# A hybrid decoder layer on one core: five queues in written order, low halves over the landed words, and first weight sums made in HBM scratch

## The chip, the cores and the metric

The kernel runs on one core of a Trainium2 chip. The metric is the device time of one launch in microseconds, as the median of several runs. A profiled execution (a span, and a row for each instruction) stands beside it.

## The reference

One decoder layer over 256 positions of 2048 features. The input is normalised and multiplied by one wide matrix, whose columns are cut into nine parts; two branches mix the positions; a gated sum of both goes through an output matrix. All of it is in float32.

```python
h = rms_norm(x, norm_g)
q, k, v, z_a, u_b, v_b, z_b, g_a, g_b = split(h @ w_in)      # 7 x 1024 and 2 x 2048 columns
q = rms_norm(q by heads of 128); k = rms_norm(k by heads of 128)
att = causal attention(q, k, v)                              # 8 heads, 256 positions
y_a = (att * silu(z_a)) @ w_proj_a
sgu = spatial_gating(gelu(u_b), gelu(v_b))                   # u * (tril(W_s) @ norm(v) + b)
y_b = (sgu * silu(z_b)) @ w_proj_b
merged = sigmoid(g_a) * y_a + sigmoid(g_b) * y_b
return x + merged @ w_out
```

## The kernel before

All weights come as 120 units of 1 MB, each 128 partitions by 2048 words, in the order of their use. A unit of the input matrix holds one pair of row blocks (the number `kp`, 0 to 7) by 1024 output columns, as four blocks of 128 x 512 that are called 12, 11, 22 and 21 and lie in that order. Blocks of units follow one another: q, k, v, za, vb, ub, zb (8 units each), then four times a block g0 to g3 (8 units: half the columns from g_a, half from g_b) and its projections (`proj`, 4 units), then out0 and out1 (8 units each).

A float32 product is made of reduced words: a value is split into a high half (`fp32r`, the word rounded) and a low half (the word minus its high half), and a product is three matmuls of 512 columns: high by low, high by high, low by high (`three`, L290). A unit is multiplied in one of two ways. *Direct*: eight block products, 24 matmuls. *By seven*: seven products of sums of blocks, as in Strassen's and Winograd's schemes, 21 matmuls, for which sums of the weight blocks (`t`) and sums of the activations (`Fx`, `Fm`, and `F4` for kp 4) are made. In `k` to `zb` and in `out` the units with kp 0 to 3 go by seven, in g0 to g3 those with kp 0 to 4; q and the projections are direct.

`split` (L128 to L157) prepares a unit on two engines. Direct: ACT casts the words to `wh` (L125), DVE subtracts, `wl` (L126). By seven: DVE makes four sums `t` (L143 two at once, L145, L146), ACT casts three blocks (`whp`, L152) and the sums (`th`, L154, two pieces), DVE subtracts for `wlp` (L155) and `tl` (L157, two pieces). The words of a unit and its sums lie in the same five buffers. In the body of unit i the kernel writes load(i+3), split(i+2), the unit's matmuls, and then the small work of the branches: norms (`sums`: ACT squares, DVE L243, POOL's power L244, and for k a multiply by `rstd` on DVE, L369), transposes, softmax, the spatial mixing, and sums out of PSUM. Loads go from SP's queue, powers and masks to POOL. ACT's and DVE's instructions stand in written order for the first eight units only; behind these, and on the other engines throughout, a scheduler sets the order.

`turn_m` turns the merged activations for `out`: PE transposes, ACT copies and casts (L490), DVE subtracts (L491). The functions:

Of the kernel before, what the change touches and what calls it, by code (L numbers as in the profile page):

```python
# [45 lines left out]
PLAIN = (0, 1, 2, 3, 4, 5, 6, 7)  # L46
NVEC = KT + 2 + H


def schedule():  # L50
    s = []

    def quad(name, c, order):
        s.extend(("quad", name, c, kp, n) for n, kp in enumerate(order))

    quad("q", 0, PLAIN)
    for name in ("k", "v", "za", "vb", "ub", "zb"):
        quad(name, 0, MIXED)
    for c in range(4):
        quad("g", c, GATE)  # L60
        s.extend(("proj", "proj", c, q, q) for q in range(4))
    for c in range(2):
        quad("out", c, OUT[c])
    return s
# [3 lines left out]
def hybrid_layer_kernel(  # L68
# [12 lines left out]

    const = ctx.enter_context(tc.tile_pool(name="const", bufs=1))
# [4 lines left out]
    psum = ctx.enter_context(tc.tile_pool(name="psum", bufs=1, space=bass.MemoryType.PSUM))  # L87

# [13 lines left out]

    raw, wh, wl, th, tl = {}, {}, {}, {}, {}

    def strassen(i):
        if i >= NG or G[i][0] != "quad" or G[i][1] == G[0][1]:
            return False
        return G[i][3] in SK or (G[i][1] == "g" and G[i][3] == 4)

# [3 lines left out]
    def new_raw(i):  # L113
        raw[i] = wpool.tile([P, WORDS], F32, tag="raw", bufs=5, name=f"raw{i}")
# [13 lines left out]
    def split(i, pieces=1, js=None):  # L128
        if i >= NG:
            return  # L130
        r = raw[i]
        if not strassen(i):
            if i not in wh:
                wh[i] = wpool.tile([P, WORDS], F32R, tag="wh", bufs=3, name=f"wh{i}")
                wl[i] = wpool.tile([P, WORDS], F32R, tag="wl", bufs=3, name=f"wl{i}")
            n = WORDS // pieces
            for j in js or range(pieces):
                sl = slice(j * n, (j + 1) * n)
                halve(wh[i][:, sl], wl[i][:, sl], r[:, sl])
            return  # L140
        t = wpool.tile([P, WORDS], F32, tag="raw", bufs=5, name=f"t{i}")
        two = t[:, 0:2 * B].rearrange("p (a n) -> p a n", a=2)
        nc.vector.tensor_tensor(two, r[:, B:3 * B].rearrange("p (a n) -> p a n", a=2),  # L143
                                r[:, None, 0:B].to_broadcast([P, 2, B]), op=ALU.add)
        nc.vector.tensor_tensor(t[:, 2 * B:3 * B], t[:, 0:B], r[:, 2 * B:3 * B], op=ALU.add)  # L145
        nc.vector.tensor_tensor(t[:, 3 * B:], t[:, 2 * B:3 * B], r[:, 3 * B:], op=ALU.add)  # L146
        wh[i] = wpool.tile([P, 3 * B], F32R, tag="whp", bufs=3, name=f"whp{i}")
        wl[i] = wpool.tile([P, 3 * B], F32R, tag="wlp", bufs=2, name=f"wlp{i}")
        th[i] = wpool.tile([P, WORDS], F32R, tag="wh", bufs=3, name=f"th{i}")
        tl[i] = wpool.tile([P, WORDS], F32R, tag="wl", bufs=3, name=f"tl{i}")  # L150
        a, b = slice(0, 2 * B), slice(2 * B, WORDS)
        nc.scalar.copy(wh[i], r[:, B:])  # L152
        for sl in (a, b):
            nc.scalar.copy(th[i][:, sl], t[:, sl])  # L154
        nc.vector.tensor_tensor(wl[i], r[:, B:], f(wh[i]), op=ALU.subtract)  # L155
        for sl in (a, b):
            nc.vector.tensor_tensor(tl[i][:, sl], t[:, sl], f(th[i][:, sl]), op=ALU.subtract)  # L157
# [7 lines left out]

    xv = const.tile([P, NVEC + S], F32, name="xv")
    vec = xv[:, 0:NVEC]
# [8 lines left out]
    nc.sync.dma_start(xv, xT[:, 0:NVEC + S])  # L176
# [3 lines left out]
    load_piece(0, 2 * B, WORDS)  # L180
    load_x(2, 4)
    load(1, pieces=2)
# [22 lines left out]
    def split_x(kp, js=None):  # L205
        i, a = kp // 4, 2 * (kp % 4)
        for j in js or range(2):
            src = xv[:, NVEC:] if kp + j == 0 else xt[i][:, a + j, :]
            nc.scalar.activation(xt[i][:, a + j, :], src, AF.Copy, scale=vec[:, 2 * kp + j:2 * kp + j + 1])
# [8 lines left out]
    nc.gpsimd.memset(mhalf, -0.5)  # L218
    ninf = const.tile([P, 1], F32, name="ninf")
# [9 lines left out]
    def load_mix():  # L229
        X["ws"] = [u(f"ws{c}") for c in range(2)]  # L230
        for c in range(2):
            t = heads(X["ws"][c])
            nc.sync.dma_start(t, wsT[:, 4 * c:4 * c + 4, :])
            nc.gpsimd.affine_select(out=t, in_=t, pattern=[[0, 4], [1, P]], base=0,
                                    channel_multiplier=-1, compare_op=ALU.is_ge, fill=0.0)
        nc.sync.dma_start(gain, bass.AP(tensor=sg.tensor, offset=sg.offset, ap=[[0, P], [1, P]]))
# [22 lines left out]

    def halves_4():  # L260
# [3 lines left out]
    def forms(src, name):  # L264
        Fs = slot(F32, f"F{name}").rearrange("p (a k t) -> p a k t", a=4, t=P)
# [28 lines left out]
    def direct(L, hs, ls, i, kp, start, stop):  # L294
# [5 lines left out]
        for c, kh in order:  # L300
# [7 lines left out]
    def seven(E, L, i, kp, first, last, started, hs, ls, Fh, Fl):  # L308
# [18 lines left out]

        for acc, (hi, lo), (bh, bl) in ((L[0], A(1, 0), W("21")), (L[1], Fm(3), W("22")), (E[0], A(0, 0), W("11")),
                                       (E[3], Fm(0), T(0)), (E[2], Fm(2), T(1)), (E[1], Fm(1), T(2)),
                                       (L[2], A(1, 1), T(3))):  # L330
            three(acc, hi, lo, bh, bl, first if any(acc is e for e in E) else not started, last and any(acc is e for e in E))

    def early(E, name, res=None):

        c11, h, c22, c12 = (u(f"{name}_{n}") for n in ("c11", "h", "c22", "c12"))
# [21 lines left out]
    def sums(C, name):  # L357
        for m in range(2):
            for c in range(2):
                ss = small.tile([P, 4], F32, tag="ss", bufs=8, name="ss")  # L360
                junk = u("junk")
                scale = rstd[:, m:m + 1] if name == "k" else 1.0
                for h in range(4):
                    nc.scalar.activation(junk[:, h * P:(h + 1) * P], C[m][c][:, h * P:(h + 1) * P], AF.Square,
                                         scale=scale, accum_out=ss[:, h:h + 1])
                rs = small.tile([P, 4], F32, tag="rs", bufs=8, name="rs")
                rsqrt(rs, ss, 4, P)
                if name == "k":
                    nc.vector.tensor_scalar(rs, rs, scale, None, op0=ALU.mult)  # L369
                X["rs", name, m, c] = rs  # L370

    def norm_qk(name):
        C = X[name]
        for m in range(2):
            for c in range(2):
                for h in range(4):
                    sl = C[m][c][:, h * P:(h + 1) * P]
                    nc.scalar.activation(sl, sl, AF.Copy, scale=X["rs", name, m, c][:, h:h + 1])

    def norm_v():  # L380
        C = X["vb"]
        for m in range(2):
            for c in range(2):
                for h in range(4):
                    sl = C[m][c][:, h * P:(h + 1) * P]
                    nc.scalar.activation(sl, sl, AF.Copy, scale=X["rs", "vb", m, c][:, h:h + 1])
                t = heads(C[m][c])
                nc.vector.tensor_tensor(t, t, gain[:, None, :].to_broadcast([P, 4, P]), op=ALU.mult)
# [372 lines left out]
```

## Time and profile before

| what | value |
|---|---|
| median of 3 runs | 660.44 us (660.41 to 662.72) |
| profiled execution | 660.26 us, of which the span is 658.5 us |
| PE busy | 650.4 us, 2980 matmuls |
| DVE busy | 606.3 us, 606 instructions |
| ACT busy | 427.8 us, 564 instructions |
| POOL busy | 25.3 us, 26 instructions |
| moved from HBM | 132.7 MB, one queue at 55.4% |

A row of the timeline gives the start, the duration, engine, line, operation and tiles, and in brackets how long the engine sat idle before it and who released it. A row of groups gives the count, the busy time in us, the mean of one in ns, and behind the second bar the idle time before. Matmuls are pipelined: the start of the next row, not the duration, is the price of one.

### The profile page before, as it was taken

How to read it: one execution, taken by the hardware profiler on the slowest of the kernel's cores; microseconds unless marked ns; L12 is line 12 of the kernel's file. 1: busy time of each engine (PE TensorE's matmuls, PEld its weight loads, DVE VectorE, ACT ScalarE, POOL GpSimd, SP SyncE). 2: the span in 40 equal slices, each digit the busy share in tenths (PEclk: the TensorE clock that was granted, in tenths of full speed). 3: DMA queues.
4: the chain of work that ended last, by engine and by line, in shares of the span. 5: the costliest groups of instructions: out<-in, count | busy, mean ns of one | idle time of the engine just before them, and what ended most of it. 6: DMA issues, size and time to landing. Idle time of an engine off the chain costs nothing.

```text
span 658.5 us, 7820 instructions
## 1 busy us (share of the span) xinstructions
PE 650.4 (99%) x2980; PEld 538.7 (82%) x2980; DVE 606.3 (92%) x606; ACT 427.8 (65%) x564; POOL 25.3 (4%) x26
## 2 busy tenths in 40 slices
PE   8999999999999999999999999999999999999997
PEld 5888887888888888888888888888888888888886
DVE  5879997999999799999999999899799979998995
ACT  7889779658886589675655755556474546746360
POOL 1002203000000003000000000000000000000000
PEclk9999999999999999999999999999999999999999
DMA  8975643652664456456449436834755483557641
GB/s 312 420 311 209 261 153 129 255 193 86 236 222 161 163 188 219 165 192 230 153 159 351 137 127 264 302 130 190 266 183 192 137 319 130 189 190 282 198 153 64
DMA packets 22213, 135.32 MB, mean 205 GB/s; under 512 B 2464, under 2 KB 3104, under 8 KB 7072
## 3 DMA queue, kind: packets, MB, share of 16 engines
q1 hardware_dynamic: 21024, 132.73, 55.4%
q10 hardware_dynamic: 1152, 2.10, 0.9%
q8 instruction: 23, 0.38, 0.2%
q14 instruction: 14, 0.11, 0.1%
HBM read 132.72 MB, written 2.10 MB: 205 GB/s over the span
## 4 chain that ended last, share of the span: by engine, by line
PE 93%; DVE 3%; POOL 1%; DMA 1%; issue 1%; ACT 0%; SPq 0%; DVEq 0%
PE acc_g L290 16%; PE y L290 13%; PE acc_out L290 9%; PE seven_g L290 8%; PE acc_q L290 6%; PE acc_vb L290 5%; PE acc_za L290 5%; PE acc_ub L290 5%; PE acc_zb L290 5%; PE acc_k L290 4%; PE seven_out L290 3%; PE acc_v L290 2%; PE seven_vb L290 2%; PE seven_zb L290 2%; PE seven_ub L290 2%; PE seven_za L290 2%
## 5 line engine op out<-in xcount | busy, mean ns | idle before, releaser
L126 DVE TENSOR_TENSOR wl<-raw,wh 128x2048 fp32r<-128x2048 f32 (+2 forms) x76 | 156.2, 2062 | 27.7 <-ACT wh L125 27.3
L154 ACT CAST th<-t 128x1024 fp32r<-128x1024 f32 x104 | 107.7, 1055 | 102.0 <-DVE t L146 35.3
L125 ACT CAST wh<-raw 128x2048 fp32r<-128x2048 f32 (+2 forms) x76 | 130.9, 1730 | 60.2 <-issue 25.3
L157 DVE TENSOR_TENSOR tl<-t,th 128x1024 fp32r<-128x1024 f32 x104 | 125.2, 1222 | 2.9 <-ACT th L154 2.9
L155 DVE TENSOR_TENSOR wlp<-raw,whp 128x1536 fp32r<-128x1536 f32 x52 | 91.0, 1750 | 1.2 <-ACT whp L152 1.2
L152 ACT CAST whp<-raw 128x1536 fp32r<-128x1536 f32 x52 | 76.8, 1482 | 23.6 <-DMA raw<-in_w 21.5
L143 DVE TENSOR_TENSOR t<-raw 128x1024 f32<-128x1024 f32 x52 | 63.3, 1218 | 1.8 <-DMA raw<-in_w 1.5
L290 PE MATMUL acc_g<-wh,xul 128*128 128x512 f32 x96 | 37.3, 389 | 0.0
L290 PE MATMUL acc_g<-wh,xuh 128*128 128x512 f32 x96 | 37.3, 389 | 0.0
L290 PE MATMUL acc_g<-wl,xuh 128*128 128x512 f32 x96 | 37.3, 389 | 0.0
L145 DVE TENSOR_TENSOR t<-t,raw 128x512 f32<-128x512 f32 x52 | 36.0, 691 | 0.2
L146 DVE TENSOR_TENSOR t<-t,raw 128x512 f32<-128x512 f32 x52 | 35.6, 685 | 0.4
L290 PE MATMUL acc_q<-wh,xuh 128*128 128x512 f32 x64 | 25.0, 391 | 1.2 <-ACT wh L125 1.2
L290 PE MATMUL acc_q<-wl,xuh 128*128 128x512 f32 x64 | 25.2, 395 | 0.3 <-DVE wl L126 0.2
L290 PE MATMUL y<-wh,zbl 128*128 128x512 f32 x64 | 25.1, 392 | 0.0
L290 PE MATMUL y<-wh,zal 128*128 128x512 f32 x64 | 25.0, 390 | 0.0
L290 PE MATMUL acc_q<-wh,xul 128*128 128x512 f32 x64 | 24.9, 390 | 0.0
L290 PE MATMUL acc_out<-wh,mh 128*128 128x512 f32 x64 | 24.9, 389 | 0.0
L290 PE MATMUL acc_out<-wl,mh 128*128 128x512 f32 x64 | 24.9, 389 | 0.0
L290 PE MATMUL y<-wl,zah 128*128 128x512 f32 x64 | 24.9, 389 | 0.0
L290 PE MATMUL y<-wh,zbh 128*128 128x512 f32 x64 | 24.9, 389 | 0.0
L290 PE MATMUL y<-wl,zbh 128*128 128x512 f32 x64 | 24.9, 389 | 0.0
(496 smaller groups left out, 1582.2 us busy)
## 6 DMA issues: line engine op xcount, KB each, us to landing
raw<-in_w SPq DMA_DIRECT2D x116, 1024.0 KB, 4.8
raw<-in_w SPq DMA_DIRECT2D x7, 512.0 KB, 8.1
xnat<-in_x SPq DMA_DIRECT2D x2, 1024.0 KB, 16.0
xres<-in_x ACTq DMA_DIRECT2D x8, 256.0 KB, 3.9
out<-out_c SPq DMA_DIRECT2D x5, 256.0 KB, 2.5
xt<-in_xT SPq DMA_DIRECT2D x2, 512.0 KB, 8.2
xt<-in_xT SPq DMA_DIRECT2D x3, 256.0 KB, 9.0
raw<-in_w SPq DMA_DIRECT2D x2, 256.0 KB, 4.3
```

Of the source, the lines that this page charges most:

```text
L125: nc.scalar.copy(h, r)
L126: nc.vector.tensor_tensor(l, r, f(h), op=ALU.subtract)
L143: nc.vector.tensor_tensor(two, r[:, B:3 * B].rearrange("p (a n) -> p a n", a=2), r[:, None, 0:B].to_broadcast([P, 2, B]), op=ALU.add)
L145: nc.vector.tensor_tensor(t[:, 2 * B:3 * B], t[:, 0:B], r[:, 2 * B:3 * B], op=ALU.add)
L146: nc.vector.tensor_tensor(t[:, 3 * B:], t[:, 2 * B:3 * B], r[:, 3 * B:], op=ALU.add)
L152: nc.scalar.copy(wh[i], r[:, B:])
L154: nc.scalar.copy(th[i][:, sl], t[:, sl])
L155: nc.vector.tensor_tensor(wl[i], r[:, B:], f(wh[i]), op=ALU.subtract)
L157: nc.vector.tensor_tensor(tl[i][:, sl], t[:, sl], f(th[i][:, sl]), op=ALU.subtract)
L290: nc.tensor.matmul(acc, a, b, start=(start and n == 0), stop=(stop and n == 2))
```

## The change

1. All five engines' queues stand in written order from the first unit to the last. Four tables set it: `SETS` (which units of a block go by seven, and the order of the eight), `LEADS` (how many units ahead a unit is split), `EVAC` and `SECOND` (when sums leave PSUM and when the second part of a turn is written), and `HOOKS` (84 entries: at which unit and at which point of it each small work is written).
2. Low halves are written over the landed words in the same bytes (an arena whose parts have two names, float32 and fp32r). Six word buffers and three sum buffers replace the five and the separate low halves. A load is written five units ahead and waits for the matmuls of the unit before the current one.
3. In g1, g2 and g3 the unit kp 5 goes by seven too (six units), in g0 only four. In out0 kp 0, 1, 2 and 4 go by seven. The activations' sums for kp 5 are `F5h` and `F5l` (`forms_5`), which out0 makes anew for its kp 4 from the turned columns (`forms_m4`, `halves_m4`).
4. The weight sums of a unit are written otherwise: the first, 12 + 11, lies in place of block 12. For the 46 units by seven of za, vb, ub, zb, g and out it is made in HBM: SP copies block 12 to one of twelve scratch tiles 13 units ahead (`pre_copy`), POOL's queue adds block 11 there with an accumulating DMA 10 units ahead (`pre_sum`), and the load takes 256 KB from scratch and 768 KB from the matrix. The other three sums are DVE rows of 512 words; ACT casts 2048 and 1536 words, DVE subtracts 2048 and 1536.
5. For k, the multiply by `rstd` is on ACT, a row of its own ahead of the norm. Unit 0's last half and unit 1 are loaded in pieces of 256 KB. The last sums out of PSUM (`early`) are written in another order.

```diff
-SK = (0, 1, 2, 3)
-MIXED = (4, 5, 0, 1, 6, 2, 3, 7)
-GATE = (5, 0, 1, 6, 2, 3, 4, 7)
-OUT = ((0, 1, 4, 2, 5, 3, 6, 7), (4, 0, 1, 5, 2, 3, 6, 7))
+SETS = {("q", 0): ((), (0, 1, 2, 4, 3, 5, 7, 6)), ("k", 0): ((0, 1, 2, 3), (4, 5, 1, 6, 0, 2, 3, 7)),
...
+        ("g", 1): ((0, 1, 2, 3, 4, 5), (0, 4, 5, 6, 3, 1, 2, 7)),
...
+        ("out", 0): ((0, 1, 2, 4), (3, 0, 1, 5, 2, 4, 6, 7)),
+        ("out", 1): ((0, 1, 2, 3), (4, 0, 5, 1, 2, 3, 6, 7))}
+SCRATCH = ("za", "vb", "ub", "zb", "g", "out")
+LEADS = {("q", 0): (3, 2, 2, 3, 3, 3, 2, 2), ("k", 0): (2, 2, 2, 2, 2, 2, 2, 2),
...
+HOOKS = [
+    ("v", 0, 2, "pre", "root", "k", 0), ("v", 0, 2, "pre", "squares", "k", 1),
...
+RAWS, WHS, THS, TS = 6, 4, 3, 3
...
+    words = [both(f"words{n}", WORDS, base + 8 * KB * n) for n in range(RAWS)]
+    sums = [both(f"sums{n}", 3 * B, base + 8 * KB * RAWS + 6 * KB * n) for n in range(TS)]
...
+    ctx.enter_context(tc.manual_schedule(engines=set(engines)))
...
+    def pre_copy(i):
+        if i < NG and strassen(i) and G[i][1] in SCRATCH:
+            pre[i] = ring[len(pre) % len(ring)]
+            nc.sync.dma_start(pre[i], w[i, :, 0:B])
+
+    def pre_sum(i):
+        if i in pre:
+            nc.gpsimd.dma_start(pre[i], w[i, :, B:2 * B], accum_op=ALU.add)
+
     def load(i, pieces=1):
...
+        if i in pre:
+            nc.sync.dma_start(raw[i][:, 0:B], pre[i])
+            load_piece(i, B, WORDS)
+            return
...
+        if i in pre:
+            nc.scalar.copy(wh[i], r)
+            mid()
+        else:
+            nc.scalar.copy(wh[i][:, B:], r[:, B:])
+            mid()
+            nc.vector.tensor_tensor(r[:, 0:B], r[:, 0:B], r[:, B:2 * B], op=ALU.add)
+            nc.scalar.copy(wh[i][:, 0:B], r[:, 0:B])
+        nc.vector.tensor_tensor(T2, r[:, 0:B], r[:, 2 * B:3 * B], op=ALU.add)
+        nc.vector.tensor_tensor(T1, T2, r[:, B:2 * B], op=ALU.subtract)
+        nc.vector.tensor_tensor(T3, T2, r[:, 3 * B:], op=ALU.add)
+        nc.scalar.copy(th[i], t)
+        late()
+        nc.vector.tensor_tensor(wl[i], r, f(wh[i]), op=ALU.subtract)
+        nc.vector.tensor_tensor(tl[i], t, f(th[i]), op=ALU.subtract)
...
+    def norm(name, n):
...
+        if name == "k":
+            nc.scalar.activation(rs, rs, AF.Copy, scale=rstd[:, m:m + 1])
...
-        if i:
-            load(i + 3)
-        split(i + 2, 2 if i < 2 else 1)
+        while i and loaded < i + RAWS - 1:
+            loaded += 1
+            load(loaded)
+        pre_copy(i + 13)
+        pre_sum(i + 10)
```

Three places show the order. In its rows a line number, the operation, and output <- inputs stand, with the number of a unit in the tile's name (`wl20` is unit 20's low half; after the change the tile is one of six, `words2`, and the unit is seen in `wh20`).

DVE in v, before, from the third quarter of k's norm to unit 20's low half:

```order
L243 TENSOR_SCALAR ms_945<-ss_938 128x4
L143 TENSOR_TENSOR t21_993<-raw21_960 128x1024
L369 TENSOR_SCALAR rs_944<-rs_944,rstd_128 128x4
L243 TENSOR_SCALAR ms_956<-ss_949 128x4
L145 TENSOR_TENSOR t21_993<-t21_993,raw21_960 128x512
L369 TENSOR_SCALAR rs_955<-rs_955,rstd_128 128x4
L146 TENSOR_TENSOR t21_993<-t21_993,raw21_960 128x512
L155 TENSOR_TENSOR wlp21_998<-raw21_960,whp21_997 128x1536
L126 TENSOR_TENSOR wl20_963<-raw20_876,wh20_962 128x2048
L157 TENSOR_TENSOR tl21_1000<-t21_993,th21_999 128x1024 x2
```

DVE at that place, after:

```order
L265 TENSOR_TENSOR words1float32r_58<-words1float32_57,wh19_932 128x2048
L266 TENSOR_TENSOR sums0float32r_92<-sums0float32_91,th19_933 128x1536
L358 TENSOR_SCALAR ms_974<-ss_926 128x4
L358 TENSOR_SCALAR ms_984<-ss_977 128x4
L230 TENSOR_TENSOR words2float32r_60<-words2float32_59,wh20_987 128x2048
L258 TENSOR_TENSOR words3float32_61<-words3float32_61 128x512
L260 TENSOR_TENSOR sums1float32_93<-words3float32_61 128x512
L261 TENSOR_TENSOR sums1float32_93<-sums1float32_93,words3float32_61 128x512
L262 TENSOR_TENSOR sums1float32_93<-sums1float32_93,words3float32_61 128x512
L265 TENSOR_TENSOR words3float32r_62<-words3float32_61,wh21_1024 128x2048
```

Unit 20's low half (L126, now L230) stood behind unit 21's sums and low half and behind two of the multiplies L369; now it stands ahead of unit 21, and the multiplies are not in this queue.

DVE in out0, before, from unit 106's low half (`ml` is a low half of the turned columns of the fourth gate block, which units with kp 4 and more need):

```order
L126 TENSOR_TENSOR wl106_4525<-raw106_4476,wh106_4524 128x2048
L491 TENSOR_TENSOR ml1_4461<-ps_mT30_4556,mh1_4460 128x4x128
L143 TENSOR_TENSOR t107_4580<-raw107_4522 128x1024
L155 TENSOR_TENSOR wlp107_4585<-raw107_4522,whp107_4584 128x1536
L491 TENSOR_TENSOR ml1_4461<-ps_mT31_4563,mh1_4460 128x4x128
L145 TENSOR_TENSOR t107_4580<-t107_4580,raw107_4522 128x512
L157 TENSOR_TENSOR tl107_4587<-t107_4580,th107_4586 128x1024
L146 TENSOR_TENSOR t107_4580<-t107_4580,raw107_4522 128x512
L126 TENSOR_TENSOR wl108_4618<-raw108_4578,wh108_4617 128x2048
L157 TENSOR_TENSOR tl107_4587<-t107_4580,th107_4586 128x1024
L143 TENSOR_TENSOR t109_4648<-raw109_4615 128x1024
```

DVE there, after, from the low halves of unit 106, which now goes by seven:

```order
L265 TENSOR_TENSOR words4float32r_64<-words4float32_63,wh106_4392 128x2048
L266 TENSOR_TENSOR sums0float32r_92<-sums0float32_91,th106_4393 128x1536
L230 TENSOR_TENSOR words5float32r_66<-words5float32_65,wh107_4428 128x2048
L397 TENSOR_TENSOR F4m_4431<-m4_4292 128x128
L398 SCALAR_TENSOR_TENSOR F4m_4431<-F4m_4431,m4_4292 128x128
L399 TENSOR_TENSOR F4m_4431<-m4_4292 128x128
L400 TENSOR_TENSOR F4m_4431<-m4_4292,F4m_4431 128x128
L260 TENSOR_TENSOR sums1float32_93<-words0float32_55 128x512
L261 TENSOR_TENSOR sums1float32_93<-sums1float32_93,words0float32_55 128x512
L262 TENSOR_TENSOR sums1float32_93<-sums1float32_93,words0float32_55 128x512
L265 TENSOR_TENSOR words0float32r_56<-words0float32_55,wh108_4459 128x2048
L266 TENSOR_TENSOR sums1float32r_94<-sums1float32_93,th108_4460 128x1536
```

Ahead of these rows stand, after the change, the two `ml` rows (L639) and three sums of unit 106; behind them come `F5l` (L677) and the five rows of unit 109. Before, units 106 and 108 were direct and the `ml` rows stood behind `wl106`.

SP's queue in v, after (before, it holds only whole loads, L111, one for each unit):

```order
L202 DMA words1float32_57<-in_w 128x2048
L221 DMA words2float32_59<-ring0_119 128x512
L202 DMA words2float32_59<-in_w 128x1536
L221 DMA words3float32_61<-ring1_120 128x512
L202 DMA words3float32_61<-in_w 128x1536
L210 DMA ring4_123<-in_w 128x512
L202 DMA words4float32_63<-in_w 128x2048
L210 DMA ring5_124<-in_w 128x512
L221 DMA words5float32_65<-ring2_121 128x512
```

POOL's queue at the same units, after (before, it holds the powers alone there):

```order
L359 TENSOR_TENSOR rs_694<-ms_695,mhalf_176 128x4
L214 DMA ring0_119<-in_w 128x512
L214 DMA ring1_120<-in_w 128x512
L359 TENSOR_TENSOR rs_973<-ms_974,mhalf_176 128x4
L359 TENSOR_TENSOR rs_983<-ms_984,mhalf_176 128x4
L214 DMA ring2_121<-in_w 128x512
L214 DMA ring3_122<-in_w 128x512
```

A load from scratch (L221) and one of 1536 words stand for a load of 2048; copies to scratch (L210) stand between loads, and POOL issues the additions (L214) between powers.

More of the change, by code (lines that the diff above doesn't have):

```diff
@@ L1 @@
+import inspect
+import re
 from contextlib import ExitStack
@@ L51, in schedule, with quad @@
     s = []
[L53 to L58, printed above, removed]
+    def quad(name, c):
+        s.extend(("quad", name, c, kp, n) for n, kp in enumerate(SETS[name, c][1]))
+    for name in ("q", "k", "v", "za", "vb", "ub", "zb"):
+        quad(name, 0)
     for c in range(4):
-        quad("g", c, GATE)
+        quad("g", c)
         s.extend(("proj", "proj", c, q, q) for q in range(4))
     for c in range(2):
-        quad("out", c, OUT[c])
+        quad("out", c)
     return s
@@ L99, in f @@
         return ap.bitcast(F32)
+    engines = (mybir.EngineType.SP, mybir.EngineType.Pool, mybir.EngineType.Activation, mybir.EngineType.DVE,
+               mybir.EngineType.PE)
+    ctx.enter_context(tc.manual_schedule(engines=set(engines)))
     raw, wh, wl, th, tl = {}, {}, {}, {}, {}
+    pre = {}
+    ring = [dram.tile([P, B], F32, tag=f"ring{n}", name=f"ring{n}") for n in range(12)]
     def strassen(i):
-        if i >= NG or G[i][0] != "quad" or G[i][1] == G[0][1]:
-            return False
-        return G[i][3] in SK or (G[i][1] == "g" and G[i][3] == 4)
+        return i < NG and G[i][0] == "quad" and G[i][3] in SETS[G[i][1:3]][0]
     def load_piece(i, a, b):
@@ L139, in split @@
                 halve(wh[i][:, sl], wl[i][:, sl], r[:, sl])
+            mid()
+            late()
             return
[L141 to L157, printed above, removed]
+        wh[i] = wpool.tile([P, WORDS], F32R, tag="wh", bufs=WHS, name=f"wh{i}")
+        th[i] = wpool.tile([P, 3 * B], F32R, tag="th", bufs=THS, name=f"th{i}")
+        t, tl[i] = sums[len(th) % TS]
+        T1, T2, T3 = (t[:, a * B:(a + 1) * B] for a in range(3))
+        if i in pre:
+            nc.scalar.copy(wh[i], r)
+            mid()
+        else:
+            nc.scalar.copy(wh[i][:, B:], r[:, B:])
+            mid()
+            nc.vector.tensor_tensor(r[:, 0:B], r[:, 0:B], r[:, B:2 * B], op=ALU.add)
[4 more added lines that the diff above has]
+        nc.scalar.copy(th[i], t)
+        late()
+        nc.vector.tensor_tensor(wl[i], r, f(wh[i]), op=ALU.subtract)
+        nc.vector.tensor_tensor(tl[i], t, f(th[i]), op=ALU.subtract)
     X = {}
@@ L179, in hybrid_layer_kernel @@
     load_x(1, 2)
-    load_piece(0, 2 * B, WORDS)
+    load_piece(0, 2 * B, 3 * B)
+    load_piece(0, 3 * B, WORDS)
     load_x(2, 4)
-    load(1, pieces=2)
+    load(1, pieces=4)
     load_x(4, 8)
@@ L292, in hybrid_layer_kernel, with direct @@
     BLK = {"12": 0, "11": 1, "22": 2, "21": 3}
-    def direct(L, hs, ls, i, kp, start, stop):
+    def direct(L, hs, ls, i, kp, start, stop, hook=None):
         t, a = kp // 4, 2 * (kp % 4)
@@ L299, in direct @@
             order = [(c, kh) for kh in range(2) for col in (1, 0) for c in (col, 2 + col)]
-        for c, kh in order:
+        for j, (c, kh) in enumerate(order):
+            if hook and j == 6:
+                hook()
             r, col = c // 2, c % 2
@@ L306, in direct, with seven @@
                   first=(i == 0))
-    def seven(E, L, i, kp, first, last, started, hs, ls, Fh, Fl):
+    def seven(E, L, i, kp, first, last, started, hs, ls, Fh, Fl, hook=None):
         a = 2 * (kp % 4)
@@ L354, in final @@
         return [[c11, c12], [h, c22]]
[L357 to L388, printed above, removed]
+    QUARTERS = ((0, 0), (1, 0), (0, 1), (1, 1))
@@ new lines, in squares, with root @@
+    def squares(name, n):
+        m, c = QUARTERS[n]
+        C = X[name][m][c]
+        ss = X["ss", name, n] = small.tile([P, 4], F32, tag="ss", bufs=8, name="ss")
+        junk = u("junk")
+        scale = rstd[:, m:m + 1] if name == "k" else 1.0
+        for h in range(4):
+            nc.scalar.activation(junk[:, h * P:(h + 1) * P], C[:, h * P:(h + 1) * P], AF.Square,
+                                 scale=scale, accum_out=ss[:, h:h + 1])
+    def root(name, n):
+        X["rs", name, n] = small.tile([P, 4], F32, tag="rs", bufs=8, name="rs")
+        rsqrt(X["rs", name, n], X["ss", name, n], 4, P)
@@ L619, in hybrid_layer_kernel @@
+    for block, c, n, when, fn, *a in HOOKS:
+        at(first[block, c] + n, fns[fn], *a, when=when)
     split_x(0, [0])
```

372 lines of the change are left out of this document (222 added, 150 removed), and 29 rows, old and new, of tables (HOOKS, LEADS, SETS).

## The prediction

> **What bounds the kernel now.** I read the page's busy times and chain first, then the list of what PE waited for, then PE's timeline at each wait and the other engines there.
>
> ```profile
> PE 650.4 (99%) x2980; PEld 538.7 (82%) x2980; DVE 606.3 (92%) x606; ACT 427.8 (65%) x564; POOL 25.3 (4%) x26
> PEclk9999999999999999999999999999999999999999
> PE 93%; DVE 3%; POOL 1%; DMA 1%; issue 1%; ACT 0%; SPq 0%; DVEq 0%
> ```
>
> ```profile
> PE acc_v L290 <- DVE wl L126: 1.3, 1, 1.3
> PE ps_w L203 <- DVE warm L200: 1.3, 1, 1.3
> PE acc_q L290 <- ACT wh L125: 1.2, 1, 1.2
> PE acc_q L290 <- DVE wl L126: 0.2, 1, 0.2
> ```
>
> PE is busy 99% of the span at full clock and 93% of the chain is PE. Its whole list of waits has four entries, three of them at the start or in the first block and one in v. So the time is the number of matmuls by their period, plus a start, a tail and two stalls. The period is read where nothing waits (first and last of 30 rows, 29 intervals):
>
> ```profile
> 205.38 0.39 PE L290 MATMUL seven_vb<-tl,Fhx 128*128 128x512 f32 x1
> ...
> 211.96 0.39 PE L290 MATMUL acc_vb<-th,xuh 128*128 128x512 f32 x1
> ```
>
> 6.58 / 29 = 0.2269 us; the second column (0.39) overlaps from row to row and is not the price. A direct unit is 24 x 0.2269 = 5.45 us, a unit by seven products 21 x 0.2269 = 4.76.
>
> DVE at 92% is the near second, so both are costed. The first stall, in v, and DVE ahead of it:
>
> ```profile
> 114.02 0.39 PE L290 MATMUL acc_v<-wh,xuh 128*128 128x512 f32 x1
> 115.73 0.51 PE L290 MATMUL acc_v<-wl,xuh 128*128 128x512 f32 x1 [1.32 <-DVE wl L126]
> 116.07 0.40 PE L290 MATMUL acc_v<-wh,xul 128*128 128x512 f32 x1
> ```
>
> ```profile
> 109.19 0.23 DVE L369 TENSOR_SCALAR rs<-rs,rstd 128x4 f32<-128x4 f32 x1 [0.90 <-POOL rs L244]
> ...
> 111.12 0.68 DVE L146 TENSOR_TENSOR t<-t,raw 128x512 f32<-128x512 f32 x1
> 111.72 1.75 DVE L155 TENSOR_TENSOR wlp<-raw,whp 128x1536 fp32r<-128x1536 f32 x1
> 113.39 2.28 DVE L126 TENSOR_TENSOR wl<-raw,wh 128x2048 fp32r<-128x2048 f32 x1
> ```
>
> ```profile
> L369 DVE TENSOR_SCALAR rs<-rs,rstd 128x4 f32<-128x4 f32 x4 | 0.9, 229 | 3.4 <-POOL rs L244 3.4
> ```
>
> Two intervals take 2.05 us instead of 0.45: 1.60 us are lost. The low half that PE waits for (unit 20, at 113.39) stands behind unit 21's sums and low half, and these behind four multiplies that each sit 0.9 us until POOL's power is done.
>
> The second stall, at unit 1, lies between these two rows (five intervals, 2.04 us instead of 1.13, so 0.91 lost), with ACT and DVE ahead of it:
>
> ```profile
> 12.04 0.39 PE L290 MATMUL acc_q<-wh,xuh 128*128 128x512 f32 x1
> ...
> 14.08 0.40 PE L290 MATMUL acc_q<-wh,xul 128*128 128x512 f32 x1
> ```
>
> ```profile
> 10.46 2.18 ACT L125 CAST wh<-raw 128x512 fp32r<-128x512 f32 x4
> 11.20 2.49 DVE L126 TENSOR_TENSOR wl<-raw,wh 128x512 fp32r<-128x512 f32 x4
> ```
>
> **The change part by part.** The sum is made against the profiled execution, 660.26 us; the median of the runs is 660.44, 0.18 above it.
>
> 1. *Fewer matmuls.* Units by seven products go from 52 to 54: g1, g2 and g3 have six instead of five, g0 four instead of five. Each saves three matmuls, 6 in all: 6 x 0.2269 = **-1.36 us**, wholly on the path as long as PE is fed.
>
> 2. *The v stall.* The order now has unit 20's low half right behind unit 19 and two small rows, ahead of unit 21; the multiply is on ACT, a unit later than the power. DVE gets back 3.4 us of waits and 4 x 0.23 of multiplies, and 4.3 us of unit 21's work no longer stand ahead: 8.6 us against the 1.60 lost. Next late would be unit 21, needed 5.45 us after unit 20, which has the same 4.3 freed. ACT takes over four small rows, each written a unit (4.76 us at least) after the power that it reads, so it doesn't wait there. **-1.60 us.** The other end, if ACT did wait 0.9 at each multiply and passed it on, is 0.
>
> 3. *DVE's work per unit.* The rows:
>
> ```profile
> L126 DVE TENSOR_TENSOR wl<-raw,wh 128x2048 fp32r<-128x2048 f32 x64 | 146.3, 2286 | 24.9 <-ACT wh L125 24.5
> L157 DVE TENSOR_TENSOR tl<-t,th 128x1024 fp32r<-128x1024 f32 x104 | 125.2, 1222 | 2.9 <-ACT th L154 2.9
> L155 DVE TENSOR_TENSOR wlp<-raw,whp 128x1536 fp32r<-128x1536 f32 x52 | 91.0, 1750 | 1.2 <-ACT whp L152 1.2
> L143 DVE TENSOR_TENSOR t<-raw 128x1024 f32<-128x1024 f32 x52 | 63.3, 1218 | 1.8 <-DMA raw<-in_w 1.5
> L145 DVE TENSOR_TENSOR t<-t,raw 128x512 f32<-128x512 f32 x52 | 36.0, 691 | 0.2
> ```
>
> Before, a unit by seven costs 1.22 + 2 x 0.69 + 1.75 + 2 x 1.22 = 6.79 us of DVE. After, with the first sum made in HBM: 3 x 0.69 + 2.29 (2048 words) + 1.75 (1536) = 6.11; without it (k and v) one 0.69 more, 6.80, no change. A direct unit costs 2.29 both times, so a sixth unit by seven adds 3.82 and five save 0.68 each: a g1-g3 block changes by 3.82 - 3.40 = +0.4. PE takes 61.9 us for each of two such blocks of before, and three matmuls, 0.68, less after, 61.2:
>
> ```profile
> 383.42:445.30 61.88, 61.88 (x275) 51.24 (x274) 59.52 (x56) 35.07 (x28) 0.00 (x0) 1.00 0.56 204
> 445.30:507.18 61.88, 61.88 (x275) 51.24 (x274) 55.41 (x51) 33.60 (x28) 0.00 (x0) 1.00 0.55 205
> ```
>
> (The columns are window, length, busy PE, PEld, DVE, ACT and POOL, clock, DMA share, GB/s.) DVE would have 59.9 and 55.8 of 61.2: still under PE. **0**; the cover is 1.3 us in the tighter block, and each further us of DVE there costs one.
>
> 4. *out0.* The order of units there makes a tight place. Let T be the start of its first unit, direct. PE needs unit 109's low half after that unit and eight transposes, two units by seven, a direct one, one by seven and two matmuls. The transposes:
>
> ```profile
> 559.05 0.60 PE L398 MATMUL ps_mT<-ident,g_c 128*128 128x128 f32 x4
> 559.49 0.60 PE L398 MATMUL ps_mT<-ident,g_h 128*128 128x128 f32 x4
> ```
>
> Four take 0.44, eight 0.88. That is T + 5.45 + 0.88 + 4.76 + 4.76 + 5.45 + 4.76 + 0.45 = T + 26.5. DVE can start unit 106 only behind the low halves of the turned columns: the transposes begin after 18 matmuls (T + 4.1), take 0.9, then ACT's copies and two DVE rows of 0.69, about T + 6.8. Then come units 106 and 108 whole (2 x 6.11), 107's low half (2.29), four small form rows, one 0.69 and unit 109 without its last row (4.36).
>
> ```profile
> L273 DVE TENSOR_TENSOR F<-xt 128x128 f32<-128x128 f32 x1 | 0.3, 284 | 0.0
> ```
>
> With 0.28 for a form row that is 12.22 + 2.29 + 1.14 + 0.69 + 4.36 = 20.7: ready at T + 27.5, 1.0 late. But rows overlap in the timeline (111.12 to 111.72 is 0.60 for a row of 0.68, 111.72 to 113.39 is 1.67 for 1.75); 18 rows with 0.09 less each take 19.1, ready at T + 25.9, in time. Ends 0 and 1.2; I take **+0.4**, nearer the spacing, which is what a queue that doesn't wait shows.
>
> 5. *The start.* Unit 1 comes in four pieces instead of two. But ACT's four casts run at 0.545 apiece without a gap, and DVE follows at 0.6, so a landing didn't set the stall: **0**. It can give at most the 0.9, and lose as much as a piece's cast, 0.5.
>
> 6. *DMA.* 46 units send 256 KB to a scratch ring, add 256 KB there from POOL's queue, and load it back in place of 256 KB; the copy and the addition come on top, 46 x 2 x 0.262 = 24.1 MB.
>
> ```profile
> q1 hardware_dynamic: 21024, 132.73, 55.4%
> raw<-in_w SPq DMA_DIRECT2D x116, 1024.0 KB, 4.8
> raw<-in_w SPq DMA_DIRECT2D x2, 256.0 KB, 4.3
> ```
>
> 132.73 MB take 55.4%, so 24.1 more take 10%, together 65%; if an addition, for which no row exists, costs twice a copy, 70%. A copy is written 3 units ahead of its addition (14.3 us) and that 5 ahead of the load (23.8) against a landing of 4.3. On SP a load waits for PE's unit i-1, and later copies stand behind it; on POOL the powers stand behind additions, each written a unit ahead of its reader. **0**; the cover is these leads.
>
> By the Trainium skill, "DMA: Bandwidth & Descriptors", section on the anatomy of a DMA on the SWDGE (gpsimd) path, a DMA from that queue takes about 2.0 us and its bytes at 436 GB/s; that makes an estimate of 2.6 us for an addition, and the sum would be the same. No run here shows it.
>
> 7. *POOL beside DVE.* The only place where both work on SBUF and DVE shows a long row:
>
> ```profile
> 196.20 2.26 POOL L234 TENSOR_SCALAR_AFFINE_SELECT ws<-ws 128x512 f32<-128x512 f32 x2 [85.25 <-ACT za_c L462]
> 195.18 2.79 DVE L157 TENSOR_TENSOR tl<-t,th 128x1024 fp32r<-128x1024 f32 x2
> 197.89 1.11 DVE L145 TENSOR_TENSOR t<-t,raw 128x512 f32<-128x512 f32 x1
> ```
>
> DVE's row of 0.69 took 1.11, 0.42 more, beside a POOL instruction of 1.13. If issuing an addition did the same, its price would lie between 0 and 1.13 us of DVE, 46 times. I take 0, as the row shows POOL computing on SBUF and an addition goes from HBM to HBM.
>
> By the Trainium skill, "SBUF — State Buffer", section "SBUF: two separate sides", the port pair of DVE and GpSimd is an exclusive lock, which a DVE operation with two SBUF inputs holds only against a GpSimd operation that reads SBUF. The trace agrees with the lock (0.42 us). The same section says that descriptors written by GpSimd are shut out while DVE runs in a two-port mode; there the DMA would be late and not DVE, and the sum stays.
>
> Sum: 660.26 - 1.36 - 1.60 + 0.4 = 657.7, and 0.18 for the median: **657.9 us**.
>
> **Rivals.**
>
> *R1, faster by over 0.5%.* The start's stall goes too (-0.9) since the smaller pieces let ACT begin earlier, and out0 holds (-0.4): 656.6. For it: the list of waits names ACT's cast there as well as DVE, and an earlier cast moves both. Against it: the casts run without a gap, so earlier words must also reach an ACT that is free earlier.
>
> *R2, the v stall only moves, or additions cost DVE the 0.42 seen.* With the stall, 659.5. With the additions: the tighter g block goes to 59.9 + 6 x 0.42 = 62.4 against 61.2, +1.2, and three additions in out0 +1.3: 660.4. For it: DVE at 92%. Against it: 8.6 us freed in v, and no SBUF in the addition.
>
> *R3, slower: each addition holds DVE.* At price x a block of g1-g3 needs 57.9 (the mean of the two) + 6x, out0 3x more: 3 x (57.9 + 6x - 61.2) + 3x over 657.9 passes 663.7 from x = 0.75 (0.5 if all blocks are like the tighter). At 1.13 it is 10.4 + 3.4 more, 671.7. For it: POOL has 26 instructions now, and nothing like these in the steady stretch. Against it: the only such row cost DVE 0.42.
>
> **How the numbers follow.** What a measurement can tell from no change is about 0.5%: below 657.1 is faster, above 663.7 slower. The forecast, with out0 between 0 and its end, has 0.53; R1 0.22, since 0.8 us separate the forecast from its bound and the start's and out0's terms together can give that; R2 0.13; R3 0.12. So faster 0.22, same 0.66, slower 0.12. The range goes from 656.0 (R1, and half of the 1.2 us that PE waits for ACT's cast in the first block) to 661.5 (R2's worst and out0's other end); R3 and the rest of R1 lie outside.
>
> **What would show it.** Right: 2974 matmuls instead of 2980; no PE wait in v; DVE rows of 0.69, 2.29 and 1.75 unchanged beside POOL's additions; the DMA share near 65%. The unit 1 stall still there at 0.9. In out0 PE waits for DVE's low half of the fifth or sixth unit by at most 1.2. Wrong: PE waits spread over g1-g3, behind DVE (R3) or behind a landing; a PE wait in v for another unit (R2); no wait at unit 1 (R1).

## The result, and the profile after

The changed kernel takes 670.62 us (median of 4 runs, 670.40 to 671.46) against 660.42: the ratio is 1.0148, 95% interval 1.0125 to 1.0172. The forecast was 657.9, within 656.0 and 661.5; what came is slower. The profiled execution took 671.46 us, 11.20 more than that of before. One execution of a later kernel, the profiled one of the first experiment, ran at a granted clock of 0.85 (726.90 us against 671.77 to 672.36 for the other three); no time below counts it, and that kernel has no period below. Three lines of the changed kernel's page, and its whole list of PE's waits:

```profile
PE 663.1 (99%) x2974; PEld 539.4 (81%) x2974; DVE 598.0 (89%) x577; ACT 425.8 (64%) x534; POOL 59.1 (9%) x72
PEclk9999999999999999999999999999999999999999
PE 98%; DMA 1%; ACT 0%; DVE 0%; SPq 0%; DVEq 0%; issue 0%
```

```profile
PE ps_w L314 <- DVE warm L311: 1.3, 1, 1.3
PE acc_q L416 <- ACT wh L229: 1.1, 1, 1.1
```

Six matmuls fewer, no wait in v, none in g or out0, full clock, 98% of the chain on PE: by these views the change did what it says. And yet PE is busy 12.7 us longer. The place to look is the spacing of the starts where nothing waits. Ten rows of PE's timeline in g1, after:

```profile
399.84 0.40 PE L416 MATMUL seven_g<-sums0float32r,xuh 128*128 128x512 f32 x1
400.07 0.39 PE L416 MATMUL acc_g<-th,xul 128*128 128x512 f32 x1
400.30 0.39 PE L416 MATMUL acc_g<-th,xuh 128*128 128x512 f32 x1
400.53 0.40 PE L416 MATMUL acc_g<-sums0float32r,xuh 128*128 128x512 f32 x1
400.77 0.39 PE L416 MATMUL acc_g<-wh,xul 128*128 128x512 f32 x1
400.99 0.39 PE L416 MATMUL acc_g<-wh,xuh 128*128 128x512 f32 x1
401.22 0.40 PE L416 MATMUL acc_g<-words4float32r,xuh 128*128 128x512 f32 x1
401.46 0.39 PE L416 MATMUL acc_g<-wh,F5l 128*128 128x512 f32 x1
401.69 0.39 PE L416 MATMUL acc_g<-wh,F5h 128*128 128x512 f32 x1
401.92 0.40 PE L416 MATMUL acc_g<-words4float32r,F5h 128*128 128x512 f32 x1
```

Nine intervals take 2.08 us, 0.231 each, where before 29 took 6.58, 0.2269. It is so from the first block to the last: behind the first 33 matmuls there are some 2670 intervals between 0.215 and 0.245 us, and their mean is 0.23166 us, before 0.22681. That is 2670 x 0.00485 = 12.95 us.

With this the difference adds up, to within the 0.2 us to which such terms can be read, from the starts of PE's rows. The last matmul starts at 665.04 instead of 654.14, +10.90. Longer period: +12.95. Six matmuls: -1.36. The v stall: -1.60. The first block: +0.75, below. A short gap in out0: +0.16 (two intervals of 0.279 and 0.334). Sum +10.9. The tail behind the last matmul adds 0.3, which brings the span to +11.2.

### The profile page after: what moved, and what is told of

It reads as the page before. It is cut to its first block, busy times and chain, and to the rows that moved or that the text cites. A ratio compares the mean times of both kernels' runs of the same rounds, so it can differ in the third digit from the quotient of the medians.

```text
span 669.7 us, 8157 instructions
## 1 busy us (share of the span) xinstructions
PE 663.1 (99%) x2974; PEld 539.4 (81%) x2974; DVE 598.0 (89%) x577; ACT 425.8 (64%) x534; POOL 59.1 (9%) x72
## 4 chain that ended last, share of the span: by engine, by line
PE 98%; DMA 1%; ACT 0%; DVE 0%; SPq 0%; DVEq 0%; issue 0%
PE acc_g L416 15%; PE y L416 13%; PE acc_out L416 9%; PE seven_g L416 9%; PE acc_q L416 7%; PE acc_k L416 5%; PE acc_v L416 5%; PE acc_vb L416 5%; PE acc_zb L416 5%; PE acc_za L416 5%; PE acc_ub L416 5%; PE seven_out L416 3%; PE seven_k L416 2%; PE seven_zb L416 2%; PE seven_vb L416 2%; PE seven_za L416 2%
## 5 line engine op out<-in xcount | busy, mean ns | idle before, releaser
L214 POOL DMA_DIRECT2D ring<-in_w x46 | 38.3, 846 | 400.4 <-DMA ring<-in_w 400.4
L263 ACT CAST th<-sums1float 128x1536 fp32r<-128x1536 f32 x18 | 26.8, 1487 | 51.3 <-DVE sums1float L262 51.3
L263 ACT CAST th<-sums0float 128x1536 fp32r<-128x1536 f32 x18 | 26.6, 1479 | 44.1 <-DVE sums0float L262 44.1
L230 DVE TENSOR_TENSOR words5float32r<-words5float,wh 128x2048 fp32r<-128x2048 f32 x14 | 32.0, 2286 | 3.6 <-ACT wh L229 3.6
L266 DVE TENSOR_TENSOR sums1float32r<-sums1float,th 128x1536 fp32r<-128x1536 f32 x18 | 31.5, 1753 | 3.2 <-ACT th L263 3.2
L230 DVE TENSOR_TENSOR words4float32r<-words4float,wh 128x2048 fp32r<-128x2048 f32 x13 | 29.7, 2287 | 4.4 <-ACT wh L229 4.4
L266 DVE TENSOR_TENSOR sums2float32r<-sums2float,th 128x1536 fp32r<-128x1536 f32 x18 | 31.5, 1752 | 0.2 <-ACT th L263 0.2
L266 DVE TENSOR_TENSOR sums0float32r<-sums0float,th 128x1536 fp32r<-128x1536 f32 x18 | 31.6, 1753 | 0.0
L265 DVE TENSOR_TENSOR words2float32r<-words2float,wh 128x2048 fp32r<-128x2048 f32 x12 | 27.5, 2292 | 1.2
L416 PE MATMUL acc_out<-wh,ml 128*128 128x512 f32 x72 | 28.3, 393 | 0.0
L230 DVE TENSOR_TENSOR words1float32r<-words1float,wh 128x2048 fp32r<-128x2048 f32 x9 | 20.6, 2287 | 5.5 <-ACT wh L229 5.5
```

The lines of the kernel that those rows point to most:

```text
L214: nc.gpsimd.dma_start(pre[i], w[i, :, B:2 * B], accum_op=ALU.add)
L230: nc.vector.tensor_tensor(l, r, f(h), op=ALU.subtract)
L263: nc.scalar.copy(th[i], t)
L265: nc.vector.tensor_tensor(wl[i], r, f(wh[i]), op=ALU.subtract)
L266: nc.vector.tensor_tensor(tl[i], t, f(th[i]), op=ALU.subtract)
L416: nc.tensor.matmul(acc, a, b, start=(start and n == 0), stop=(stop and n == 2))
```

## Experiments

Three theories were set against each other: the address of an operand matters (A); traffic and writes in place slow PE's reads (B); waits in PE's queue (C). Addresses and offsets are worked out from the sizes of the tiles, in the order in which the kernel makes them; the traces hold none. In a matmul of this kernel the stationary operand is a tile of activations and the moving operand, of 512 columns, a tile of weights.

**All operands on multiples of 64 bytes.** In the kernel before every operand of a matmul starts on a multiple of 64; in the changed one the activations and high halves start 32 past it.

```diff
-    rstd = const.tile([P, 2], F32, name="rstd")
-    ssum = const.tile([P, 2], F32, name="ssum")
+    pair = const.tile([P, 4], F32, name="pair")
+    rstd, ssum = pair[:, 0:2], pair[:, 2:4]
```

> The changed kernel with rstd and ssum in one tile of the const pool, so that every later tile starts 32 bytes lower and every operand of a matmul starts on a multiple of 64 bytes, as in the kernel before; nothing else differs. Theory A (matmul operands that start 32 bytes past a multiple of 64 lengthen the issue period from 0.2267 to 0.2317 us): about 2650 matmuls get 0.005 us back, 13 us, so about 657.5 us, and the steady rows show 0.2267 again. Rival B (20% more DMA traffic and low halves written over the landed words slow PE's reads): no change, 670.6 us. Rival C (waits between matmuls in PE's queue): no change, 670.6 us.

671.78 us, ratio 1.0173 (1.0156 to 1.0190): no gain.

**The kernel before, shifted as a whole** by the same edit:

> The kernel before with rstd and ssum in one tile of the const pool, so that every later tile starts 32 bytes lower: nearly all matmuls then have both operands 32 bytes past a multiple of 64. Nothing else differs. Theory A: about 2670 matmuls at 0.2317 us or a little more instead of 0.2267, 13 us or more, so 673 us or above. Rivals B and C: no change, 660.4 us.

660.59 us, ratio 1.0001 (0.9992 to 1.0010), mean period 0.2268. Theory A in this form is dead: with both operands 32 bytes past a multiple of 64 the period is that of before.

**Only stationary, or only moving operands off the line:**

```diff
     small = ctx.enter_context(tc.tile_pool(name="small", bufs=4))
+    wpool.tile([P, 8], F32, tag="gap", bufs=1, name="gap")
```

(in the changed kernel, with three buffers instead of four for the small tile `mx`; and in the kernel with the one-tile edit above)

> The changed kernel with 32 bytes set in ahead of the casts of the weights (and one small buffer fewer), so that the moving operands (wh, th, low halves) all start on a multiple of 64 and only the stationary ones (activations) stay 32 past it. Theory A1 (the moving operand's address costs): about 657.5 us. Theory A2 (the stationary operand's address costs): about 670 us. Both: between, 661 to 668. Rivals B and C: 670.6 us.

> The changed kernel with all stationary operands on a multiple of 64 and the high halves and high sums of the weights (two thirds of the moving operands) 32 bytes past it. Theory A1 (the moving operand's address costs): about 670 us. Theory A2 (the stationary operand's address costs): about 657.5 us. Rivals B and C: 670.6 us.

675.42 us (ratio 1.0225, 1.0208 to 1.0242) and 671.15 (1.0172, 1.0144 to 1.0200); mean periods in the profiled executions 0.2333 and 0.2330. Each was expected to be fast under one half of theory A, and neither is. The first has a *longer* period than the changed kernel; so had the second in its profiled execution, which took 674.89 us, while its other three took 670.56 to 671.32. What made that one longer no run shows. What the two kernels share with it, and what the shifted kernel of before lacks, is that the two operands of a matmul stand at different offsets to each other: 32 and 288 bytes (modulo 512) in the one, 32 and 320 in the other, 288 for the low halves and sums in the changed kernel, 320 for these in the kernel aligned to 64. In the kernel before, shifted or not, all are 0. That this offset between the two operands sets the period is theory D, and it was tested in both directions.

**The changed kernel with equal offsets.** Instructions and their order are the same; only addresses move.

```diff
-    mhalf = const.tile([P, 8], F32, name="mhalf")
+    mhalf = const.tile([P, 80], F32, name="mhalf")
...
-        ss = X["ss", name, n] = small.tile([P, 4], F32, tag="ss", bufs=8, name="ss")
+        ss = X["ss", name, n] = small.tile([P, 4], F32, tag="ss", bufs=4, name="ss")
...
-        X["rs", name, n] = small.tile([P, 4], F32, tag="rs", bufs=8, name="rs")
+        X["rs", name, n] = small.tile([P, 4], F32, tag="rs", bufs=4, name="rs")
...
-            mx = small.tile([P, 4], F32, tag="mx", name="mx")
+            mx = small.tile([P, 4], F32, tag="mx", bufs=3, name="mx")
```

> The changed kernel with 288 bytes set in ahead of the activations (and four buffers each instead of eight for two small tiles, three instead of four for a third), so that both operands of every matmul start at the same byte modulo 512, as in the kernel before; the instructions and their order are the same. Theory D (the period depends on the two operands' offset to each other: a matmul reads its moving operand while the next one's stationary operand is read): period 0.2267 us again, 657 to 659 us. Theory E (it depends on where the low halves lie, over the landed words, on the written order or on the traffic): 670 to 672 us.

659.61 us, ratio to before 0.9984 (0.9974 to 0.9993): 11 us under the changed kernel, 0.6 above the time expected, and the only version that is under both. PE's rows, the first and last of 30, with 29 intervals in 6.57 us, 0.2266 each:

```profile
399.70 0.39 PE L416 MATMUL acc_g<-words5float32r,xuh 128*128 128x512 f32 x1
...
406.27 0.39 PE L416 MATMUL seven_g<-th,Fhx 128*128 128x512 f32 x1
```

The place of the low halves, the written order, the traffic and PE's queue are here what they are in the changed kernel, so theory E, B and C are out as causes of the longer period. The next kernels go the other way: they move tiles in the kernel before.

**The kernel before with a gap ahead of its low halves**, 72 words (288 bytes), then 16 (64), 32 (128) and 64 (256):

```diff
                 wh[i] = wpool.tile([P, WORDS], F32R, tag="wh", bufs=3, name=f"wh{i}")
+                if i == 0:
+                    wpool.tile([P, 72], F32, tag="gap", bufs=1, name="gap")
```

> The kernel before with a gap of 288 bytes ahead of the low halves, so that 1220 of 2916 matmuls (low halves, and the weights' halves of units by seven) have operands 288 bytes apart modulo 512, as the low halves have in the changed kernel. Theory D: the period rises towards 0.2315 us, 670 to 674 us. Theory E: no change, 660.4 us.

> The kernel before with a gap of 64 bytes ahead of the low halves. Theory D with a unit of 64 bytes or less: no change, 660.4 us; with a larger unit: 670 us or more. Theory E: 660.4 us.

> The kernel before with a gap of 128 bytes ahead of the low halves. With a unit of 128 bytes (offsets of 32, 64 and 288 lengthened the period): no change, 660.4 us. With a larger unit: 670 to 674 us.

> The kernel before with a gap of 256 bytes ahead of the low halves. With a unit of 128 or 256 bytes: no change, 660.4 us. With a unit of 512 bytes: 670 to 674 us.

**The kernel before with 288 bytes ahead of all weight tiles**, so that the moving operands agree with one another and not with the stationary ones (the gap at the start of `wpool`):

> The kernel before with a gap of 288 bytes ahead of all its weight tiles, so that every moving operand of the weights (landed words' high and low halves and sums alike) starts 288 bytes modulo 512 from the stationary operand, and all moving operands agree with one another. Theory D1 (offset between the moving and the stationary operand): the period rises to 0.231 to 0.2335 us, 671 to 678 us. Theory D2 (offset between one moving operand and the next): 0.2267 us, 660.4 us.

The rows of PE in g1 with all moving operands 288 off, and with the low halves 256 off, first and last of 30 each:

```profile
399.78 0.39 PE L291 MATMUL seven_g<-th,Flx 128*128 128x512 f32 x1
...
406.55 0.40 PE L291 MATMUL seven_g<-tl,Fhx 128*128 128x512 f32 x1
```

```profile
399.73 0.39 PE L292 MATMUL acc_g<-wl,xuh 128*128 128x512 f32 x1
...
406.30 0.39 PE L292 MATMUL seven_g<-th,Fhx 128*128 128x512 f32 x1
```

6.77 and 6.57 us for 29 intervals. All together (the period is the mean of all intervals between 0.215 and 0.245 us in the profiled execution; counts are of some 2850 matmuls, the transposes left out, where one expectation above has 2916; each ratio is to runs of before made beside it, with medians from 660.42 to 660.62 us):

| kernel | offset of moving to stationary operand | period, us | time, us | ratio to before |
|---|---|---|---|---|
| before | 0 | 0.2268 | 660.4 | 1 |
| before, all shifted by 32 | 0 | 0.2268 | 660.59 | 1.0001 |
| before, low halves by 256 | 256 for 1220 | 0.2268 | 660.82 | 1.0006 (0.9995 to 1.0018) |
| before, low halves by 64 | 64 for 1220 | 0.2318 | 672.65 | 1.0182 (1.0162 to 1.0203) |
| before, low halves by 288 | 288 for 1220 | 0.2317 | 672.03 | 1.0174 (1.0159 to 1.0189) |
| before, low halves by 128 | 128 for 1220 | 0.2327 | 675.33 | 1.0223 (1.0193 to 1.0253) |
| before, all moving by 288 | 288 for 2724 | 0.2333 | 676.51 | 1.0241 (1.0211 to 1.0270) |
| after | 288 for 906 | 0.2317 | 670.62 | 1.0148 (1.0125 to 1.0172) |
| after, equal offsets | 0 | 0.2268 | 659.61 | 0.9984 (0.9974 to 0.9993) |

So it is the offset between the moving and the stationary operand (D1), not between one moving operand and the next (D2). It is free at 0 and 256 bytes and costs at 64, 128 and 288: of the powers of two, only 256 fits as the unit. The kernel with 32 bytes ahead of the casts fits too: all its weight tiles are 32 off modulo 256 (32 and 288), and its period, 0.2333, is that of the kernel with all moving operands 288 off. The kernel with 128 came out 1.3 us above its expectation, the others of this group within theirs.

The price is not in proportion: a third of the matmuls off (after) costs three quarters of what nearly all cost. The starts show why. In the changed kernel every third matmul reads a low half and is off; the interval that begins with it is 0.2349 us on average, the one ahead of it 0.2313, and the third 0.2287, against 0.2267 to 0.2269 for all three in the kernel before. Matmuls whose own operands agree thus pay beside one whose operands don't. That two reads of one memory meet when a matmul streams its words while the next weights are loaded would fit, but no run here shows what meets; nor can these kernels tell whether a matmul's own stationary operand counts or the next one's, since all stationary operands have the same offset.

**No sums in HBM.** `SCRATCH = ()`, once in the changed kernel and once with equal offsets; copies, additions and the extra loads are gone, and DVE makes the first sums.

> The changed kernel with no sums in HBM: the 46 copies, additions and 256 KB loads are gone, DVE makes the first sum in place (46 rows of 0.69 us more) and ACT casts in two pieces. If DMA traffic or POOL's additions lengthened the period: 0.2267 us again, 658 us plus what DVE then lacks in g1 to g3 (6 x 0.69 = 4.1 a block against about 1.3 to 5 us of slack). Theories D and E without traffic: period still 0.2315 to 0.2333, 670 to 674 us.

> The kernel with equal offsets (f1_same_offset) and no sums in HBM: DVE makes all first sums. If POOL's additions and the traffic cost nothing and DVE has the slack that the prediction gave, 660 us plus at most 6 x 0.69 - 1.3 = 2.8 us in each of g1 to g3, at most 668 us; if DVE in written order has no slack elsewhere either, as its waits in the kernel without scratch at the long period suggest (21 us of PE gaps), 675 to 685 us.

689.62 us (ratio to before 1.0438, 1.0423 to 1.0454, period still 0.2318) and 686.31 (1.0389, 1.0359 to 1.0419, period 0.2270). Without additions and their traffic, too, the period is what the addresses make it. The scratch is worth much: with equal offsets, 26.7 us. DVE there is busy 628.8 us instead of 597.4, 31.4 more for 46 sums, and most of it comes out as PE waiting: behind the first block, PE's intervals over 0.245 us hold 29.2 us beyond the period, with scratch 3.0. The page's busy times without scratch and the first lines of PE's waits, and then the page's busy times with scratch, both with equal offsets:

```profile
PE 658.7 (96%) x2974; PEld 540.1 (79%) x2974; DVE 628.8 (92%) x623; ACT 432.2 (63%) x580; POOL 21.5 (3%) x26
```

```profile
PE seven_g L416 <- DVE g_h L685: 4.4, 3, 1.7
PE seven_g L416 <- DVE g_c L683: 2.4, 2, 1.3
PE acc_zb L416 <- DVE words0float32r L265: 2.1, 1, 2.1
```

```profile
PE 649.8 (99%) x2974; PEld 537.2 (82%) x2974; DVE 597.4 (91%) x577; ACT 425.5 (65%) x534; POOL 59.6 (9%) x72
```

Both came out above their expectations (689.62 where 670 to 674 was expected, 686.31 where 675 to 685 was the worse case). The slack beside DVE was put too high, and looked for in g1 to g3 alone. By the first starts of each block's matmuls, those three blocks take 3.9, 2.4 and 4.7 us longer without scratch, where at most 2.8 was expected, and za to zb take 11.9 longer (5.3 of it in zb), out 4.7, g0 nothing. Of the seventeen entries in that run's list of PE's waits all but two name DVE; ACT's casts come in two pieces there, and what that adds was not taken apart.

## Why the prediction was wrong

**The step that failed is the first:** "the time is the number of matmuls by their period", with the period taken from before, 0.2269, as if it were the chip's. It was the property of a layout in which all tiles lie at equal offsets modulo 256, and the change moves the tiles. The arena with words and sums (66 KB) now stands first, behind it the small tiles of `const` (5856 bytes, each tile rounded up to 32), then the activations and the casts. 66 KB is a multiple of 512 and 5856 is 224 past one, so the low halves and sums in the arena stand 512 - 224 = 288 bytes, modulo 512, from the activations. No term of the sum was for that, and none of the three rivals. It came to +12.95 us, where the whole difference at the last matmul is +10.90.

Where the period is restored (equal offsets), the other steps can be read one by one. Its profiled execution took 659.25 against 660.26: -1.0 where -2.6 was forecast. That its median, 659.61, is close to the 659.5 that R2 had for a v stall that only moves is luck: the v stall did move, but 1.05 of its 1.60 us were still gained, and out0, the start and the tail together took about as much away. PE's waits there:

```profile
PE ps_w L314 <- DVE warm L311: 1.3, 1, 1.3
PE acc_q L416 <- ACT wh L229: 1.1, 1, 1.1
PE acc_q L416 <- DVE cut_float32r L230: 0.6, 3, 0.2
PE acc_out L416 <- DVE words1float32r L265: 0.3, 1, 0.3
PE acc_v L416 <- DVE words4float32r L265: 0.3, 1, 0.3
```

- *Fewer matmuls, -1.36:* 2974 rows instead of 2980, as said.
- *The v stall, -1.60:* unit 20's stall is gone; unit 22 now waits (R2, the stall moves):

```profile
124.84 0.39 PE L416 MATMUL acc_v<-wh,xuh 128*128 128x512 f32 x1
125.50 0.50 PE L416 MATMUL acc_v<-words4float32r,xuh 128*128 128x512 f32 x1 [0.27 <-DVE words4float32r L265]
125.84 0.39 PE L416 MATMUL acc_v<-wh,Flx 128*128 128x512 f32 x1
```

  Two intervals of 1.00 instead of 0.45, 0.55 lost, so -1.05. In the changed kernel itself nothing waits there, since PE is later.
- *out0, +0.4 (0 to 1.2; the prediction's own working gives 1.0 for the upper end):* at the place named, unit 109's low half, PE loses 0.57:

```profile
596.28 0.39 PE L416 MATMUL acc_out<-wh,mh 128*128 128x512 f32 x1
596.97 0.50 PE L416 MATMUL acc_out<-words1float32r,mh 128*128 128x512 f32 x1 [0.30 <-DVE words1float32r L265]
```

  (0.69 instead of 0.23, and 0.11 more behind it.)
- *The start, 0:* unit 1's stall stays, against R1; unit 2 loses 0.6 more (the three waits on `cut` are those of units 1 and 2). The term was +0.6 with equal offsets. The tail, which had no term, is 0.3 longer.
- *DVE's rows:* 0.69, 2.29 and 1.75, as taken, also beside the additions. From the changed kernel, two groups of DVE, POOL's additions, and one pair that overlaps:

```profile
L265 DVE TENSOR_TENSOR words2float32r<-words2float,wh 128x2048 fp32r<-128x2048 f32 x12 | 27.5, 2292 | 1.2
L266 DVE TENSOR_TENSOR sums2float32r<-sums2float,th 128x1536 fp32r<-128x1536 f32 x18 | 31.5, 1752 | 0.2 <-ACT th L263 0.2
L214 POOL DMA_DIRECT2D ring<-in_w x46 | 38.3, 846 | 400.4 <-DMA ring<-in_w 400.4
```

```profile
405.80 1.75 DVE L266 TENSOR_TENSOR sums2float32r<-sums2float,th 128x1536 fp32r<-128x1536 f32 x1
406.13 0.81 POOL L214 DMA_DIRECT2D ring<-in_w  x1 [7.16 <-DMA ring<-in_w]
```

  So R3, the rival that had the right sign, did not happen: an addition is a POOL row of 0.85 us and costs DVE nothing. The ten rows of L266 that overlap an addition take 1.753 us on average, the 44 others 1.753. The Trainium skill, "SBUF — State Buffer", section "SBUF: two separate sides", has the lock, for a DVE operation with two SBUF inputs, only against a GpSimd operation that reads SBUF; the trace agrees for an addition that goes from HBM to HBM (1.753 us beside it).
- *DMA, 65 to 70%:* low. The additions' queue takes far more for each byte than the other:

```profile
q1 hardware_dynamic: 34704, 144.80, 60.2%
q0 software_dynamic: 6624, 12.06, 12.3%
```

```profile
ring<-in_w SPq DMA_DIRECT2D x46, 256.0 KB, 6.6
ring<-in_w POOLq DMA_DIRECT2D x46, 256.0 KB, 6.9
```

  72.5% together; an addition costs 1.02% for a MB against 0.42%, 2.5 times a plain transfer. It landed after 6.9 us, where the prediction estimated 2.6; the copies to scratch took 6.6 in the same run, so this is hardly the adding alone. The leads cover it: POOL waits for the copies, and no row waits for an addition.

The terms of the sum were thus right in kind, and 1.6 us too hopeful in all; what was wrong by 13 us was the price of a matmul.

## What to carry to other kernels

Before a change that moves tiles, compare the start addresses of the two operands of the hot matmuls, before and after, modulo 256: here 64 bytes ahead of the low halves cost 1.8%, and 288 bytes more in one small tile far away took 1.6% off. When PE is the bound, its list of waits is empty and its clock is full, read the spacing of the starts; a longer period shows in no wait. And a price taken from a steady stretch is a price of that layout, to be bounded when the layout changes.

## What the runs showed of the hardware

- The issue period of a 128 x 512 fp32r matmul was 0.2268 us with both operands at equal offsets modulo 256, and up to 0.2333 without. The Trainium skill, "TensorE: Matmul & The Clock Gate", section "Wait — 56ns, not 53.3ns?", has start to start at N / 2.4 GHz and about 2.5 ns, 215.7 ns for N = 512, with nothing on addresses; the measured rows decide here, and both values lie above it.
- In some executions the first matmuls behind the warm-up start 0.43 us apart, and only then 0.23. That this is the clock, granted late, fits: the trace's records of the granted clock begin at 10.23 us in the changed kernel, and at 4.49 us in the kernel before, whose first rows are not slow. After, nine rows (first and last):

```profile
6.55 0.63 PE L416 MATMUL acc_q<-wh,xul 128*128 128x512 f32 x1
...
9.96 0.53 PE L416 MATMUL acc_q<-wh,xuh 128*128 128x512 f32 x1
```

  8 intervals in 3.41 us. It costs less than it looks, since unit 1's stall then vanishes: the 33rd matmul behind the warm-up starts at 15.46 instead of 14.55, 0.91 later, of which about 0.15 is the longer period. The kernel before, shifted by 32 bytes, also started slowly (first and last of nine rows) and still took 660.05 us in its profiled execution:

```profile
6.73 0.63 PE L290 MATMUL acc_q<-wh,xul 128*128 128x512 f32 x1
...
10.15 0.63 PE L290 MATMUL acc_q<-wh,xuh 128*128 128x512 f32 x1
```

  Of the seven profiled executions with before's instructions five started so, and of the five with the changed kernel's instructions three, so the slow start is not the change's.
